# One queue for the loads after the first pair, the rows of w and u behind the first k, and the fill's state operations ahead of later sums, in an RWKV WKV kernel

## Chip, cores, metric

The kernel runs on one core of one Trainium2 chip. The metric is the device time of one execution in microseconds (us), lower is better. A run gets a state: on one core, "slow" is a run more than 1.5% above the fastest run of the same kernel. Ratios use fast runs alone.

## The reference

```python
# w, u: [256]; k, v: [16, 2048, 256] float32
for b in range(16):
    aa, bb, pp = 0, 0, -1e38
    for t in range(2048):
        kk, vv = k[b, t], v[b, t]
        ww = u + kk;  qq = max(pp, ww)
        e1, e2 = exp(pp - qq), exp(ww - qq)
        output[b, t] = (e1 * aa + e2 * vv) / (e1 * bb + e2 + 1e-8)
        ww = pp - w + kk;  qq = max(ww, kk)
        e1, e2 = exp(ww - qq), exp(kk - qq)
        aa, bb, pp = e1 * aa + e2 * vv, e1 * bb + e2, qq
```

## The kernel before

The sequence is cut into 16 chunks of 128 steps; a "pair" is four batches of one chunk, 128x1024 elements of k and as many of v (1.05 MB together), and there are 64 pairs. For each pair, VectorE rounds k (`km`), TensorE makes logarithms of weights from it and from w and u (`logs`), ScalarE takes exponentials into a ring (`exps`, L187 for the first nine pairs, the wide L189 after), and VectorE multiplies by v (`times_v`). The outputs come LAG = 9 pairs later: `den`, `recip`, `num`, `mult`, `store`. Beside this a state is carried from chunk to chunk: `sums` of four pairs, `copy_sums`, `turn`, logarithms `LL`, offsets, weights `G`, a product `CB`, `turn_back`, and `inject`, which copies the state (`cb`) with a small transfer `EZR<-cb` into one row of the ring, where `den` of the next chunk reads it. The loop's first nine slots, which fill the ring, are "the fill".

```python
    RING = 12; AHEAD = 6; LAG = 9
    ...
    for n in range(3):
        load(n, SP, SP)                    # k and v of pairs 0 to 2 in the SP queue
    for r, g0, x in ((0, 0, w), (1, 2, u)):
        K(SC.dma_start(out=wuf...))        # w and u in the ACT queue
    ...
    for n in range(3, AHEAD):
        load(n)                            # pairs 3 to 5, and later ones, in the POOL queue
    ...
    def inject(c):
        cb = small.tile([128, 128], BF16, tag="cb", name="cb")
        K(DVE.tensor_copy(cb, st.pop((c, "CT"))))
        r0 = 4 * c % RING
        for q in range(2):
            row = EZR[HS - 1:128:HS, 2 * q, r0, 0, 0:1]
            K(SP.dma_start(
                out=bass.AP(tensor=row.tensor, offset=row.offset, ap=[list(row.ap[0]), [1, 4 * 2 * D]]),
                in_=cb[HS * q:HS * q + HS, :]))
    ...
    for n in range(LAG):                   # the fill
        load(n + AHEAD)
        exps(n)
        logs(n + 1)
        if n:
            sums(n - 1)
        small_work(n, "act")               # state operations of this slot
        small_work(n, "nums")
        small_work(n, "pe")
        idle_matmuls(4, NUMB)
        small_work(n, "mid")
        small_work(n, "chain")
        times_v(n)
        cast_v(n + 1)
        round_k(n + 2)
    for n in range(LAG, NP):               # the steady part
        ...
```

## Time and profile before

| | before |
|---|---|
| time, median of 4 runs | 329.76 us (328.05 to 333.73) |
| span of the profiled run | 324.6 us |
| start to the first wide exponential (pair 9) | 54.73 us |
| from there to the second | 8.06 us |
| second to last wide exponential, 53 pairs | 229.15 us |
| last one to the end | 32.66 us |

The starts of the wide exponentials (128x2048, one per pair) are the best ruler of this kernel: they cut a run into fill, steady part and tail, and a gap of much more than 4.4 us between two of them is a stop. The granted clock was 1.00 until 20 us, 0.64 and 0.68 in the two stretches of 5 us from 20 to 30, 1.00 from 30 to 40 and 0.60 to 0.71 from 40 to 60; a matmul on k (L176, NLE) took 0.71 us near 23 and 46 us, and 0.46 from 9 to 15.

### The profile page before, as it was taken

The page shows a single profiled execution, that of the slowest core. Times are in us where ns is not written, and L with a number is a line of the kernel's source. Part 1 is how long each engine was busy: PE and PEld are TensorE (multiplying, and loading weights), DVE is VectorE, ACT ScalarE, POOL GpSimd, SP SyncE. Part 2 cuts the span into 40 slices and gives each one's busy share as a digit, 9 for nine tenths or more (in the row PEclk, how much of TensorE's full clock was granted, in tenths as well). Part 3 has the DMA queues.
Part 4 walks back from the last instruction along what each step waited for, and adds up shares of the span by engine and source line. Part 5 has one row for each costly group of instructions (what it writes and reads, how often), then busy time and mean ns, then how long its engine had stood idle before and what let it go on. Part 6 is the DMA issues. An engine that isn't in the chain of part 4 may idle for free.

```text
span 324.6 us, 4795 instructions
## 1 busy us (share of the span) xinstructions
PE 280.6 (86%) x1684; PEld 130.2 (40%) x1716; DVE 273.4 (84%) x547; ACT 258.7 (80%) x251; POOL 147.2 (45%) x204
## 2 busy tenths in 40 slices
PE   7839687899969999999989989898989999998781
PEld 2323343344434444444444444343434444444230
DVE  4835547599969999999999999999999999998652
ACT  1524543599868998989898989999898989898792
POOL 8824135046435454555553736364555543121231
PEclk9987957899998999999999999999999999999998
DMA  7999966469998999999999999999999999433566
GB/s 240 351 349 348 335 191 157 173 206 284 364 360 298 275 327 387 310 398 292 397 352 388 301 368 355 378 320 366 369 364 357 327 391 317 144 129 135 204 241 207
DMA packets 37914, 97.85 MB, mean 301 GB/s; under 512 B 5238, under 2 KB 16002, under 8 KB 37890
## 3 DMA queue, kind: packets, MB, share of 16 engines
q0 software_dynamic: 32016, 93.34, 86.2%
q1 hardware_dynamic: 5568, 3.93, 4.0%
q8 instruction: 13, 0.21, 0.3%
q10 hardware_dynamic: 306, 0.27, 0.3%
q14 instruction: 11, 0.09, 0.1%
HBM read 67.12 MB, written 33.55 MB: 310 GB/s over the span
## 4 chain that ended last, share of the span: by engine, by line
PE 60%; DVE 20%; DMA 12%; ACT 3%; issue 2%; SPq 1%; DVEq 0%; POOL 0%; ACTq 0%
PE PS L176 22%; PE PS L329 14%; DVE EZR L207 9%; PE PS L316 8%; DVE ot L335 8%; PE PS L171 7%; DMA vr<-in_v_dram 5%; DMA EZR<-cb 5%; PE PS L228 5%; ACT rd L322 2%; PE PS L372 2%; DMA kr<-in_k_dram 2%; PE PS L245 1%; DVE km L162 1%; DVE vb L202 1%
## 5 line engine op out<-in xcount | busy, mean ns | idle before, releaser
L340 POOL DMA_DIRECT2D out_dram<-ot x63 | 47.7, 757 | 143.3 <-DVE ot L335 84.1
L189 ACT ACTIVATE EZR<-PS 128x2048 bf16<-128x2048 f32 x55 | 102.7, 1867 | 10.7 <-PE PS L176 10.2
L335 DVE TENSOR_TENSOR ot<-PS,rd 128x512 f32<-128x512 f32 (+1 forms) x119 | 85.9, 724 | 15.6 <-PE PS L329 10.4
L207 DVE TENSOR_TENSOR EZR<-EZR,vb 128x2048 bf16<-128x2048 bf16 x64 | 78.3, 1224 | 4.3 <-ACT EZR L187 4.3
L322 ACT ACTIVATE rd<-PS 128x1024 f32<-128x1024 f32 (+1 forms) x65 | 65.5, 1007 | 8.4 <-PE PS L316 6.3
L324 ACT ACTIVATE rd<-rd 128x1024 f32<-128x1024 f32 (+1 forms) x65 | 68.0, 1046 | 2.0
L329 PE MATMUL PS<-EZR,LN 128*128 128x512 bf16 x126 | 48.2, 383 | 12.8 <-DVE ot L335 12.5
L176 PE MATMUL PS<-km,NLE 128*128 128x512 f32 x128 | 49.3, 467 | 10.6 <-DVE km L162 10.4
L61 POOL DMA_DIRECT2D kr<-in_k_dram x61 | 46.2, 758 | 20.9 <-DVE km L162 13.3
L162 DVE CAST km<-kr 128x1024 fp32r<-128x1024 f32 x64 | 47.2, 738 | 0.1
L316 PE MATMUL PS<-EZR,L 128*128 128x512 bf16 x127 | 37.9, 379 | 7.4 <-ACT rd L322 3.0
L176 PE MATMUL PS<-km,NLZ 128*128 128x512 f32 x128 | 41.9, 409 | 0.0
L69 POOL DMA_DIRECT2D vr<-in_v_dram x47 | 38.5, 819 | 6.0 <-DVE vb L202 5.2
L202 DVE CAST vb<-vr 128x1024 bf16<-128x1024 f32 x50 | 35.5, 710 | 5.2 <-DMA vr<-in_v_dram 5.2
L329 PE MATMUL PS<-EZR,IdN 128*128 128x512 bf16 x102 | 38.8, 381 | 0.2 <-issue 0.2
L316 PE MATMUL PS<-EZR,Id 128*128 128x512 bf16 x128 | 38.1, 379 | 0.1
L171 PE MATMUL PS<-WU,CO 32*128 32x512 f32 x256 | 34.5, 513 | 1.1 <-ACT EZR L189 0.4
L187 ACT ACTIVATE EZR<-PS 128x1024 bf16<-128x1024 f32 x18 | 17.4, 1022 | 22.4 <-PE PS L176 22.4
L176 PEld LDWEIGHTS PS<-km,NLE 128*128 128x128 f32 x128 | 20.1, 197 | 27.4 <-issue 13.9
L176 PEld LDWEIGHTS PS<-km,NLZ 128*128 128x128 f32 x128 | 25.2, 197 | 6.3
L228 PE MATMUL PS<-EZR,OH 128*32 128x256 bf16 x512 | 26.4, 284 | 0.0
L171 PEld LDWEIGHTS PS<-WU,CO 32*128 32x128 f32 x256 | 13.0, 187 | 30.3 <-issue 7.4
(58 smaller groups left out, 204.1 us busy)
## 6 DMA issues: line engine op xcount, KB each, us to landing
out_dram<-ot POOLq DMA_DIRECT2D x63, 512.0 KB, 6.5
kr<-in_k_dram POOLq DMA_DIRECT2D x61, 512.0 KB, 8.1
vr<-in_v_dram POOLq DMA_DIRECT2D x47, 512.0 KB, 8.8
vb<-in_v_dram POOLq DMA_DIRECT2D x14, 256.0 KB, 7.8
kr<-in_k_dram SPq DMA_DIRECT2D x3, 512.0 KB
vr<-in_v_dram SPq DMA_DIRECT2D x3, 512.0 KB
EZR<-cb SPq DMA_DIRECT2D x32, 16.0 KB
out_dram<-ot SPq DMA_DIRECT2D x2, 128.0 KB
```

What stands on the lines that cost most here:

```text
L61: K((kq or POOL).dma_start(out=kr, in_=src[0]))
L162: K(DVE.tensor_copy(km, kr_of.pop(n)))
L171: K(PE.matmul(half(n, q)[:, i, :], CO[g:g + 32, :], WU[g:g + 32, :], start=True, stop=False, tile_position=(g, 0), skip_group_check=True))
L176: K(PE.matmul(half(n, q)[:, i, :], (NLE, NLZ)[q], km[:, i, :], start=False, stop=True, skip_group_check=True))
L189: K(SC.activation(ez(n)[:, 0:2], PS[:, 0:4, :].rearrange("p (q i) x -> p q i x", q=2), ACT.Exp))
L207: K(DVE.tensor_mul(ez(n)[:, 2:4], ez(n)[:, 0:2], vb.unsqueeze(1).broadcast_to([128, 2, 2, D])))
L316: K(PE.matmul(DENB[:, i, :], mats[m], ez(n)[:, q, i, :], start=q == 0, stop=q == 1, skip_group_check=True))
L322: K(SC.activation(rd[:, i, :], DENB[:, i, :], ACT.Ln, scale=RS))
L324: K(SC.activation(rd[:, i, :], rd[:, i, :], ACT.Exp, scale=-1.0))
L329: K(PE.matmul(bank, mats[m], ez(n)[:, q, i, :], start=q == 2, stop=q == 3, skip_group_check=True))
L335: K(DVE.tensor_mul(o[:, i, :], bank, rd[:, i, :]))
L340: K(POOL.dma_start(out=out[4 * p:4 * p + 4, c * TC:(c + 1) * TC, :].rearrange("n t d -> t n d"), in_=OT.pop(n)))
```

## The change

The intent: deliver the first pairs in the order in which they are wanted, start the first pair earlier, and let the state's operations of the fill go before sums that they do not need. The diff, cut:

```diff
-    for n in range(3):
-        load(n, SP, SP)
-    for r, g0, x in ((0, 0, w), (1, 2, u)):
-        K(SC.dma_start(out=wuf...))
+    K(POOL.memset(wuf, 0.0))              # was on DVE
+    load(0, SP, SC)
+    load_row(SP, 0, 0, w)
+    load_row(SP, 1, 2, u)
     ... selects and iotas on POOL ...
-    for n in range(3, AHEAD):
+    for n in range(1, 3):
         load(n)
     ... selects of Lx and Sel, now behind these loads ...
+    for n in range(3, AHEAD):
+        load(n)
+    def out_matrices():                   # Id, IdN, L, LN: made at the end of slot 0
@@ the plan of the last chunk
-                    (s + 2, "pe", turn_back), (s + 2, "last", inject)]
+                    (s + 3, "turn", turn_back), (s + 3, "first", inject)]
@@ the fill
-        if n:
+        if n and n % 4 == 0:
             sums(n - 1)
         small_work(n, "act")
         small_work(n, "nums")
+        small_work(n, "mid")
+        small_work(n, "chain")
+        if n % 4:
+            sums(n - 1)
         small_work(n, "pe")
         idle_matmuls(4, NUMB)
-        small_work(n, "mid")
-        small_work(n, "chain")
         times_v(n)
@@ the tail
         small_work(n, "turn")
+        small_work(n, "first")
```

More of the change, by code (lines that the diff above doesn't have):

```diff
@@ L91, with load_row @@
     Sel = consts.tile([128, 3, 2, 2, 4, 2], F32, tag="Sel", name="Sel")
+    def load_row(eng, r, g0, x):
+        K(eng.dma_start(out=wuf.rearrange("(g r) n d -> r g n d", r=32)[r, g0:4], in_=bass.AP(
+            tensor=x.tensor, offset=x.offset, ap=[[0, 4 - g0], [0, 2], list(x.ap[0])])))
+    K(POOL.memset(wuf, 0.0))
     fill(M1, -1.0)
-    fill(wuf, 0.0)
-    for n in range(3):
-        load(n, SP, SP)
-    for r, g0, x in ((0, 0, w), (1, 2, u)):
-        K(SC.dma_start(out=wuf.rearrange("(g r) n d -> r g n d", r=32)[r, g0:4], in_=bass.AP(
-            tensor=x.tensor, offset=x.offset, ap=[[0, 4 - g0], [0, 2], list(x.ap[0])])))
+    fill(I1, 0.0)
+    load(0, SP, SC)
+    load_row(SP, 0, 0, w)
+    load_row(SP, 1, 2, u)
     K(SC.preload_act_table_set("natural_log_exp_and_others"))
-    fill(I1, 0.0)
     fill(idle, 0.0)
-    fill(Lx, 1.0)
     select(M1, GE, 0.0, -1, -1, [[1, 128]])
@@ L110 @@
         select(COf, NE, 1.0, -32 * g - 1, 1, [[0, 128]])
-    select(Lx, GE, 0.0, -1, -1, [[1, 128]])
-    for h in range(2):
-        select(Lx, NE, 1.0, -(HS * h + HS - 1), 1, [[0, 128]])
-    for n in range(3, AHEAD):
+    for n in range(1, 3):
         load(n)
@@ L123 @@
     K(DVE.tensor_tensor(NLZ, NLE, I1, ALU.add))
+    fill(Lx, 1.0)
     fill(Sel, 0.0)
-    for j, r in ((0, 0), (1, 8), (2, 64)):
-        for h in range(2):
-            select(Sel[:, j, h], NE, 1.0, -r - h, 1, [[-16, 2], [-2, 4], [-32, 2]])
     fill(OH, 0.0)
@@ L132 @@
     K(DVE.tensor_copy(CO, COf))
+    select(Lx, GE, 0.0, -1, -1, [[1, 128]])
     for h in range(2):
-        fill(Lx[HS * h:HS * h + HS, HS * (1 - h):HS * (2 - h)], 0.0)
-    mats = {}
-    for name, x, f in (("Id", I1, 1.0), ("IdN", I1, RS), ("L", Lx, 1.0), ("LN", Lx, RS)):
-        mats[name] = matrix(name, BF16)
-        K(DVE.tensor_single_scalar(mats[name], x, f, op=ALU.mult))
-    mats["OH"], mats["Sel"] = OH, Sel.rearrange("p a h n c i -> p (a h) n (c i)")
-    WU = consts.tile([128, D], F32R, tag="WU", name="WU")
-    K(DVE.tensor_copy(WU, wuf.rearrange("p n d -> p (n d)")))
+        select(Lx, NE, 1.0, -(HS * h + HS - 1), 1, [[0, 128]])
+    for j, r in ((0, 0), (1, 8), (2, 64)):
+        for h in range(2):
+            select(Sel[:, j, h], NE, 1.0, -r - h, 1, [[-16, 2], [-2, 4], [-32, 2]])
+    for n in range(3, AHEAD):
+        load(n)
+    WU = consts.tile([128, D], F32R, tag="WU", name="WU")
+    mats = {"OH": OH, "Sel": Sel.rearrange("p a h n c i -> p (a h) n (c i)")}
+    def out_matrices():
+        for h in range(2):
+            fill(Lx[HS * h:HS * h + HS, HS * (1 - h):HS * (2 - h)], 0.0)
+        for name, x, f in (("Id", I1, 1.0), ("IdN", I1, RS), ("L", Lx, 1.0), ("LN", Lx, RS)):
+            mats[name] = matrix(name, BF16)
+            K(DVE.tensor_single_scalar(mats[name], x, f, op=ALU.mult))
     EZR = consts.tile([128, 4, RING, 2, D], BF16, tag="EZR", name="EZR")
@@ L374 @@
     idle_matmuls(16, MISC)
+    K(DVE.tensor_copy(WU, wuf.rearrange("p n d -> p (n d)")))
     round_k(0)
@@ L395 @@
         round_k(n + 2)
+        if n == 0:
+            out_matrices()
     for n in range(LAG, NP):
```

## The prediction

> **What bounds the kernel now.** I read the page first: VectorE (DVE), TensorE (PE) and ScalarE (ACT) are each busy for 80 to 86% of the span, so no average names a bound. The stretches do.
>
> ```profile
> 10.00:15.00 5.00, 4.16 (x21) 1.84 (x19) 3.98 (x10) 3.88 (x4) 4.01 (x7) 1.00 1.05 348
> 15.00:20.00 5.00, 2.76 (x19) 1.28 (x20) 1.06 (x1) 1.94 (x2) 1.50 (x2) 1.00 1.05 349
> ...
> 50.00:55.00 5.00, 2.67 (x17) 1.23 (x13) 4.78 (x7) 0.55 (x2) 2.87 (x2) 0.71 0.52 102
> ...
> 60.00:65.00 5.00, 3.46 (x23) 1.13 (x22) 2.08 (x4) 4.20 (x5) 0.00 (x0) 1.00 0.25 87
> ...
> 140.00:180.00 40.00, 37.28 (x242) 17.16 (x247) 38.95 (x77) 36.69 (x35) 20.59 (x28) 1.00 1.05 364
> ```
>
> Columns: length, busy time of PE, weight loads, DVE, ACT, POOL, granted clock, DMA share, GB/s. From 100 to 290 us DVE is busy for about 98%, one pair costs 4.28 us (the 128x2048 exponentials start 17.1 us apart per four), and nothing in that loop is edited. The fill, up to the first 128x2048 exponential at 54.73 us, is different: DVE idles there while the DMA engines are saturated at 350 GB/s until 40 us, and then the DMA engines idle too (102 and 87 GB/s). So the fill is first starved by loads and later by something else. The waits up to 66 us name both:
>
> ```profile
> DVE nF L256 <- ACT LL L250: 5.6, 2, 3.6
> DVE vb L202 <- DMA vr<-in_v_dram: 5.2, 1, 5.2
> DVE cb L302 <- PE PS L296: 3.3, 1, 3.3
> DVE WU L141 <- DMA wuf<-in_u_dram: 2.3, 1, 2.3
> ACT LL L250 <- PE PS L228: 1.8, 1, 1.8
> DVE tb L276 <- PE PS L228: 1.6, 1, 1.6
> ```
>
> (total us, times, longest.) The chain that ended last passes through the second of these, and the timeline shows its end:
>
> ```profile
> 3.85 17.44 DMA vr<-in_v_dram
> ...
> 17.41 0.51 PE L171 MATMUL PS<-WU,CO 32*128 32x512 f32 x4
> 21.31 0.69 DVE L202 CAST vb<-vr 128x1024 bf16<-128x1024 f32 x1 [5.25 <-DMA vr<-in_v_dram]
> 22.66 1.22 PE L176 MATMUL PS<-km,NLE 128*128 128x512 f32 x2 [4.74 <-DVE km L162]
> ```
>
> The v of pair 2 lands at 21.3 us. By then some 350 GB/s x 18.8 us = 6.6 MB had moved, over six pairs of 1.05 MB, because pairs 0 to 2 go in one queue and 3 to 5 beside them in another: bandwidth goes to data not yet wanted. A last place is in the tail, where PE, in its order, waits for the last state product:
>
> ```profile
> 302.30 0.40 PE L296 MATMUL PS<-Id,CB 128*128 128x128 bf16 x4 [1.31 <-DVE CB L280]
> 303.65 1.22 DVE L335 TENSOR_TENSOR ot<-PS,rd 128x1024 f32<-128x1024 f32 x1 [0.63 <-PE PS L329]
> 304.97 1.02 ACT L322 ACTIVATE rd<-PS 128x1024 f32<-128x1024 f32 x1 [1.59 <-DVE ot L335]
> ```
>
> [...] the sixth transfer of the first queue (3.1 MB in all) lands only when 6.6 MB have moved. [...] LL reads the turned sums in one half of a bank and still waits for the next sums (L228) written to the other half, 1.8 us. [...] Here a load costs POOL 0.75 us typically and up to 1.1, so I count it as a risk of tenths. [...]
>
> **The change, part by part.**
>
> *Start.* k0 alone heads the SP queue, w and u follow at once, v0 is alone in the ACT queue, and pairs 1 and up are issued by POOL. k0 and v0 together are 1.05 MB, 3.0 us from the first data at about 2.5 us: landed at about 5.5 to 6. w and u, 12 KB, ride behind: about 6.3. WU (0.57, at 8.30 before) is then ready at about 6.9 and km0 (0.72) at 7.5; the first L176 matmul, 9.57 before, comes at about 7.5. The wuf memset moves to POOL; at 0.48 us on DVE, I allow 0.5 to 1 there, ahead of 1.9 us of selects and iotas. Loads of pairs 1 and 2 leave POOL between about 3.3 and 6.3 us (four of 0.75), when k0 and v0 still flow; pair 3 leaves at about 10, and data for 2.5 + 3 x 3.0 = 11.5 us is queued by then. So no gap in the data.
>
> *One queue in order.* Pair n now lands at about 2.5 + 3.0(n+1): v2 at 11.5 to 12.5 and k3 at 13 to 14, where DVE had v2 at 21.3. From there the slot takes the larger of DMA 3.0, DVE 1.22 + 0.69 + 0.69 = 2.6 and PE in its order: rows 0.51, steps 1.35, sums 0.40, four idle matmuls 1.04 and gaps, 3.36 as between 27.03 and 30.39 us. Walking the slots: DVE has times_v(0) at 10.1, v1 and k2 cast by 12.4, the four output matrices moved there 1.15 (as at 4.86 to 6.0), times_v(1) at 13.5, k3 rounded at 15.9, k4 at 18.3. PE's steps for pairs 3, 4, 5 then start at 15.9, 19.2 and 22.6, the last two by 3.36. Before, those of pair 5 started at 30.82: 8.2 us saved, of which I count 7.5, as k4 and k5 land within a microsecond of being wanted.
>
> *State ahead of later sums.* In slot 5, LL no longer waits for L228: 1.8 us, all of it on the way LL, offsets, times_v, rounding of k7, since DVE sat 3.6 us for LL. In slot 6, tb loses its 1.6 us; it may pay some of it to G, whose exponential ends about 0.4 us after exps(6): 1.5 counted. In slot 7, turn_back only passes one set of sums, 0.5 us; the rest of cb's 3.3 us is logs(8), which stays ahead. Slot 8 keeps its old order: 0. Sum 3.8. PE's clock adds something: with no 4.7 us hole before pair 3, matmuls that ran 1.4 to 1.5 times longer near 23, 46, 52 and 56 us may run full; 1.0 counted of a possible 2.5.
>
> *Tail.* The four matmuls of pair 56 (0.88 us) go ahead of turn_back, into the 1.31 us in which PE waits for CB. cb is still ready at about 303.0, so the multiplication at 303.65 can come at about 303.0, and the reciprocals behind it, which wait for it, move with it: 0.6.
>
> Sum: 7.5 + 3.8 + 1.0 + 0.6 = 12.9 us. Part of it is given back below.
>
> **The rivals.** (a) *The steady part pays it back.* It needs 97.85 MB / 64 = 1.53 MB per 4.28 us, 357 GB/s[...], and the slack of the DMA engines between 40 and 75 us is worth some 16 us by the GB/s row (5.7 MB below 350). The earlier start uses 12 of it. The state's small transfer EZR<-cb then lands later: it took 9.6 us at 85.8 and cost one slot 3.4 us (exponentials 7.78 instead of 4.38 apart). One or two more such stops would leave 6 to 9 us of the gain, 322 to 325 us. Against: in steady state loads are issued some six pairs ahead and land within 7 to 9 us, without growth from 120 to 260 us, and slot 9 is long enough (8 us, one pair of loads) for the backlog to drain. I take off 0.9 for it. (b) *The fill becomes compute-bound at once*: with the idle matmuls at 3.36 us per slot, PE and not loads then sets it, and any landing delay adds. If slots 1 to 5 took 4.0 instead of 3.4, the gain would be 9 to 10, so 321. (c) *The loads were hidden anyway and the gain is nil*: then the chain would not have 17.44 us on v2 with DVE idle for 5.2 and all engines at zero between 18 and 20 us. I give this 2%. (d) *POOL issues too late*, after memset and selects: each microsecond of gap in the data costs as much; at most 2.
>
> **Range and chances.** 330.8 - 12.9 + 0.9 = 318.8 us, called 319. If all goes well (clock 2.5, full 8.2, a stop of 3.4 gone) 312 to 313; if (a) comes fully, 325. The three runs of before spread over 5.7 us, which is most of the rest. Faster by over 2% means below 324.2, a gain of 6.6, half of what I count: 0.88. Within 2%: 0.11. Slower by over 2%: 0.01.
>
> **What would show it right or wrong.** Right: v2 lands by 13 us and the wait of 5.2 us for it is gone; the first L176-kind matmul before 8.5; the first 128x2048 exponential at 41 to 44 us instead of 54.73; waits of LL and tb for sums gone; 350 GB/s until about 40 us and a shorter dip after it; 4.28 us per pair as before; the span from the last rows matmul to the end shorter by about 0.6. Wrong: the first such exponential after 47 (the fill has another bound), or on time but with new waits for EZR<-cb, pairs over 4.4 us apart or DVE waiting for loads after 60 us (rival a), or the first data gap between 6 and 12 us (rival d).

## The result, and the profile after

The changed kernel takes 320.57 us, median of 4 runs (318.93 to 333.11), against 329.76; it and all kernels below gave correct results. The ratio is 0.972, 95% interval 0.965 to 0.979: the mean time of this kernel's fast runs over that of the other's of the same rounds, so not quite the ratio of the medians. It is faster by 2.8%, about 9 us, and the median lies within 2 us of the predicted 319.

The run with the first profile was a slow one (333.11 us). So the same kernel was profiled again on another chip (e1 below); that run was fast, 314.81 us. Its stretches, with the columns as before (length, PE, weight loads, DVE, ACT, POOL, clock, DMA share, GB/s):

```profile
10.00:15.00 5.00, 4.28 (x28) 2.15 (x27) 4.49 (x10) 3.37 (x5) 4.98 (x9) 1.00 1.02 329
15.00:20.00 5.00, 4.69 (x31) 2.18 (x29) 4.54 (x7) 2.85 (x3) 5.00 (x5) 1.00 1.00 346
50.00:55.00 5.00, 4.09 (x25) 1.74 (x24) 4.02 (x9) 4.97 (x6) 1.29 (x2) 0.97 0.69 238
60.00:65.00 5.00, 4.84 (x35) 2.48 (x34) 5.00 (x7) 4.92 (x7) 3.00 (x5) 1.00 1.02 276
140.00:180.00 40.00, 37.74 (x250) 17.58 (x249) 39.26 (x77) 37.08 (x35) 21.66 (x29) 1.00 1.05 365
```

From 15 to 20 us DVE is now busy for 4.54 of 5 us instead of 1.06, at the same 346 to 349 GB/s: the same traffic, in a useful order. The steady stretch has not changed. The waits of the first 55 us of the same run (total us, times, longest), with those for v of pair 2 and of LL and tb for the sums gone:

```profile
DVE WU L378 <- DMA wuf<-in_u_dram: 2.8, 1, 2.8
PE PS L319 <- DMA EZR<-cb: 2.8, 1, 2.8
DVE nF L259 <- ACT LL L253: 2.6, 2, 1.7
...
DVE cb L305 <- PE PS L299: 1.5, 1, 1.5
```

The second of these lines is new. The timeline of the same run shows it at the end of the fill:

```profile
7.69 0.73 PE L179 MATMUL PS<-km,NLE 128*128 128x512 f32 x2
...
22.18 0.73 PE L179 MATMUL PS<-km,NLE 128*128 128x512 f32 x2
...
35.67 1.12 SPq L309 DMA_DIRECT2D EZR<-cb  x2
...
40.49 1.87 ACT L192 ACTIVATE EZR<-PS 128x2048 bf16<-128x2048 f32 x1
...
46.86 1.01 PE L319 MATMUL PS<-EZR,L 128*128 128x512 bf16 x2 [2.81 <-DMA EZR<-cb]
...
48.76 1.02 ACT L325 ACTIVATE rd<-PS 128x1024 f32<-128x1024 f32 x1 [6.23 <-PE PS L319]
```

The first matmul on k comes at 7.69 us (9.57 before), the one of pair 5 at 22.18 (30.82), the first wide exponential at 40.49 (54.73): the fill is 14.2 us shorter. But the first state, issued at 35.67, lands only at 46.8, PE waits for it before the first output, and the second wide exponential comes 10.29 us after the first, instead of 8.06.

Cut at the wide exponentials, in us ("four copies" is e2 and e4, explained below):

| stretch | before | after, fast (e1) | after, slow | before, four copies (e4) | after, four copies (e2) |
|---|---|---|---|---|---|
| to the first | 54.73 | 40.49 | 40.97 | 56.08 | 40.79 |
| first to second | 8.06 | 10.29 | 9.98 | 8.06 | 6.51 |
| second to last | 229.15 | 230.09 | 248.20 | 225.54 | 225.14 |
| last to the end | 32.66 | 32.23 | 32.25 | 32.52 | 31.76 |
| span | 324.6 | 313.1 | 331.4 | 322.2 | 304.2 |

The fill of the slow run is as short as that of the fast one. All that the slow run loses, 18.1 us, lies between the second and the last wide exponential. There, six gaps of 6.6 to 8.2 us stand among gaps of about 4.4, at every eighth pair. The waits of the slow run, over its whole span:

```profile
PEld L319 <- DMA EZR<-cb: 21.1, 8, 3.7
PE PS L319 <- DMA EZR<-cb: 19.8, 8, 3.3
```

and of the fast one:

```profile
PE PS L319 <- DMA EZR<-cb: 8.0, 3, 2.8
...
PEld L319 <- DMA EZR<-cb: 6.2, 2, 3.2
```

(Weight loads and matmuls of one stop both have a line; they are not to be added.) So the two runs differ by the number of stops for the state's small transfer, and the question is what that transfer waits for.

### The profile page after: what moved, and what is told of

It is laid out like the page before. It is cut to its first block, busy times and chain, and to the rows that moved or that the text cites.

```text
span 331.4 us, 4824 instructions
## 1 busy us (share of the span) xinstructions
PE 282.1 (85%) x1716; PEld 128.5 (39%) x1716; DVE 273.7 (83%) x546; ACT 260.0 (78%) x251; POOL 152.8 (46%) x209
## 2 busy tenths in 40 slices
DMA packets 36378, 97.85 MB, mean 295 GB/s; under 512 B 5238, under 2 KB 13954, under 8 KB 36354
## 4 chain that ended last, share of the span: by engine, by line
PE 48%; DMA 29%; DVE 14%; ACT 4%; issue 2%; POOL 0%; DVEq 0%; SPq 0%; ACTq 0%; POOLq 0%
DMA EZR<-cb 26%; PE PS L179 14%; PE PS L332 12%; PE PS L319 11%; DVE EZR L210 5%; PE PS L174 5%; DVE ot L338 5%; PE PS L231 4%; ACT rd L325 3%; DMA kr<-in_k_dram 2%; DMA wuf<-in_u_dram 1%; ACT EZR L190 1%; DVE km L165 1%; DVE vb L205 1%; PE PS L248 1%
## 5 line engine op out<-in xcount | busy, mean ns | idle before, releaser
L319 PE MATMUL PS<-EZR,L 128*128 128x512 bf16 x128 | 40.3, 398 | 22.7 <-DMA EZR<-cb 19.8
L332 PE MATMUL PS<-EZR,LN 128*128 128x512 bf16 x128 | 50.2, 392 | 10.6 <-DVE ot L338 9.8
L61 POOL DMA_DIRECT2D kr<-in_k_dram x63 | 49.7, 789 | 6.9 <-DVE km L165 1.9
L179 PE MATMUL PS<-km,NLE 128*128 128x512 f32 x128 | 47.9, 456 | 4.4 <-DVE km L165 4.2
L332 PE MATMUL PS<-EZR,IdN 128*128 128x512 bf16 x128 | 49.8, 389 | 0.0
L165 DVE CAST km<-kr 128x1024 fp32r<-128x1024 f32 x64 | 48.5, 760 | 0.0
L179 PE MATMUL PS<-km,NLZ 128*128 128x512 f32 x128 | 41.0, 402 | 0.0
L319 PE MATMUL PS<-EZR,Id 128*128 128x512 bf16 x128 | 40.4, 399 | 0.0
L190 ACT ACTIVATE EZR<-PS 128x1024 bf16<-128x1024 f32 x18 | 17.4, 1021 | 14.4 <-PE PS L179 14.4
L319 PEld LDWEIGHTS <-L 128*128 128x128 bf16 x128 | 12.0, 99 | 40.9 <-DMA EZR<-cb 21.1
L179 PEld LDWEIGHTS PS<-km,NLE 128*128 128x128 f32 x128 | 19.4, 191 | 21.4 <-issue 14.8
```

The costliest lines, as they stand in the source:

```text
L61: K((kq or POOL).dma_start(out=kr, in_=src[0]))
L165: K(DVE.tensor_copy(km, kr_of.pop(n)))
L179: K(PE.matmul(half(n, q)[:, i, :], (NLE, NLZ)[q], km[:, i, :], start=False, stop=True, skip_group_check=True))
L319: K(PE.matmul(DENB[:, i, :], mats[m], ez(n)[:, q, i, :], start=q == 0, stop=q == 1, skip_group_check=True))
L332: K(PE.matmul(bank, mats[m], ez(n)[:, q, i, :], start=q == 2, stop=q == 3, skip_group_check=True))
```

## The experiments

Two theories of the stops were open. M: an inject lands late because of its shape, two copies of two partitions each, 128 packets of 256 B in all. Q: the transfer lands late since there is a backlog of loads, however it is cut. And there was a rival to stops altogether, R: the steady part is slower for another reason.

### e1: the changed kernel again

> The changed kernel as it is, once more, to get a profile of a fast run (the first profile fell in a slow one: 331.4 us, with the first wide exponential at 40.97 us instead of 54.73 but six stops of 3 to 4 us for EZR<-cb). Theory S (stops): the fill keeps its gain of 13.8 us in every run, and runs differ only by the number of stops for EZR<-cb: a fast run of 318 us has two or three of them (7 to 9 us), since 324.6 - 13.8 - 0.6 would be 310. Rival R (the steady part is slower for another reason): a fast run has no more than the one stop that the kernel before had, and the missing 8 us are spread over pairs of more than 4.28 us or lie in the tail.

Measured: 314.81 us in the profiled run, where S had 318 for a fast one; the timed ones 320.29, 323.94 and 324.14. The profile has three stops (second gap 10.29; later 6.22 and 6.38 us), the steady gaps are 3.94 to 4.54 as ever, and the tail is 0.4 us shorter. Theory S holds, R falls. That the other three runs have more stops is likely from their times, but they have no profile.

### e2: the inject as four copies of one partition

```diff
         for q in range(2):
-            row = EZR[HS - 1:128:HS, 2 * q, r0, 0, 0:1]
-            K(SP.dma_start(out=bass.AP(..., ap=[list(row.ap[0]), [1, 4 * 2 * D]]),
-                           in_=cb[HS * q:HS * q + HS, :]))
+            for h in range(2):
+                p = HS * h + HS - 1
+                row = EZR[p:p + 1, 2 * q, r0, 0, 0:1]
+                K(SP.dma_start(out=bass.AP(..., ap=[list(row.ap[0]), [128, 32], [1, 128]]),
+                               in_=cb[HS * q + 32 * h:HS * q + 32 * h + 32, :]))
```

> The changed kernel with the state's small transfer EZR<-cb issued as four copies of one partition (32 rows of 256 B) instead of two copies of two partitions. Theory M [...] lands in 2 to 4 us instead of 7 to 11. Then no stop is left and the time is 308 to 312 us in every run. Rival Q (backlog): the transfer lands late because all DMA engines have a backlog of loads and stores, however it is cut; then the stops stay, or grow a little as the last of four copies is issued 1 us later, and the time stays at 319 to 321 or above. Rival R: no stop to take away, 318 to 321.

Measured: 306.33 us median (305.37 to 307.07), all four runs within 0.6%; ratio to the kernel before 0.927 (0.918 to 0.936). (The record's rule classes the ratios of e2, e3, e4, e7, e9 and e10 as unclear; here the slowest run of e2 is 21 us below the fastest of the seven runs of the kernel before in the same rounds.) No stop is left in the profile (waits for EZR<-cb: 0.2 us in all), the second gap is 6.51 us. M's time was met and passed, and as the cause of the stops Q falls. One number of M was missed: the copies land 5.4 us after their issue in the median, not the estimated 2 to 4.

```profile
DMA to landing us min/median/max: 1.8/5.4/6.5
```

The packets can be counted on the page. The first of these lines is of the slow run of the changed kernel, the second of e2:

```profile
DMA packets 36378, 97.85 MB, mean 295 GB/s; under 512 B 5238, under 2 KB 13954, under 8 KB 36354
```

```profile
DMA packets 37338, 97.85 MB, mean 322 GB/s; under 512 B 6198, under 2 KB 14914, under 8 KB 37314
```

Both move the same 128 packets of 256 B per inject, and e2 has 960 more packets under 512 B, of 4 B in the trace. On how many DMA engines a copy ran is not shown. What the records do show is the packets' times. From the start of the first of an inject's 128 packets to the end of the last, in us, in order (taken from the packet records of the trace):

```
after, fast (e1):  8.7 1.7 1.9 2.2 1.9 1.6 1.9 1.8 1.6 4.0 7.3 1.9 8.0 1.1 1.1 1.1
after, slow:       8.2 1.4 8.4 1.3 7.1 1.7 8.1 6.0 8.0 5.1 8.0 2.0 7.9 1.1 1.1 1.2
after, e2:         2.7 2.1 2.5 4.6 2.5 3.0 2.6 2.4 3.0 3.2 2.5 2.4 3.6 2.1 (the last two run together)
```

With the two copies an inject's packets mostly take either about 1 to 2 us, or 7 to 9 us (4.0, 5.1 and 6.0 also occur), and the three stops of e1 belong to the three entries above 7. By its own record a small packet takes 0.018 us (median), and a 4096 B packet of the loads 0.18 (mean): 128 small ones add to 2.3 us, so most of 8 us is not their own time. In the first long one of e1, from 39.99 to 45.9 us, 63 small packets start, mostly in twos about 0.2 us apart. That is about the time of one packet of the loads and one small one (0.18 and 0.018 us), but what a small packet waits for is not shown, since the records do not name the engine.

The same records say when an inject is long. During the injects of 5 us and more, 16.1 to 17.4 packets of loads and stores are in flight on the average; during those of up to 2.7 us, at most 15.5 (all 48 injects of the profiles before, after slow and e1; the one of 4.0 us has 15.6). So the long ones are those with more traffic in flight. Why there is less at one inject than at the next is not shown.

One part of the delay does not depend on the shape. The first small packet starts 4.3 us after the issue in e1 (35.67 to 39.99 us) and 4.4 us in e2 (35.89 to 40.33), when 336 GB/s are moved, but 1.4 us in the kernel before at 49.19, when 203 are (49 to 51 us). Most of the 5.4 us that e2's copies still take is this part, which M had left out.

### e3: one more pair of delay

```diff
-    LAG = 9
+    LAG = 10
-    TURNS = 9
+    TURNS = 10
```

> The changed kernel with the outputs one pair further behind (LAG and TURNS 10 instead of 9), so that EZR<-cb has 4.3 us more before it is wanted. Theory S: stops of 3 to 4 us vanish, for one more pair in the fill and one more in the tail instead of one in the steady part (estimate 2.9 + 2.15 - 4.28 = +0.8 us): 310 to 313 us. Rival R: nothing but the +0.8: 319 to 322.

Measured: 308.80 us (307.44 to 309.92), no wait for EZR<-cb in the list of waits, no gap over 4.6 us after the twelfth pair. So the stops vanish either by landing sooner (e2) or by waiting later (e3). It is 2.5 us behind e2 (means 308.74 and 306.28), more than the 0.8 estimated; the tail alone is 34.0 instead of 31.8 us.

### e4: the kernel before with the four copies

> The kernel before with the same four copies as in e2. Theory M: its stop of 3.4 us at pair 18 and those that its slower runs have vanish: 321 to 323 us (profiled span about 321) and a small spread. The difference to e2 is then the change without its stops: 13.8 in the fill, 0.6 in the tail and the 2 us that the slot of the first outputs lost, 12 to 15 us. Rival Q: 328 to 331 as before.

Measured: 320.29 us median; fast runs 317.80, 319.84, 320.73 (mean 319.5), and a profiled run of 323.86 that counts as slow. No stop is in the profile. So the kernel before loses to the shape of the copies as well: its fast runs on that chip have a mean of 330.4. That all of these 11 us were stops is likely, not shown, since its one profile has a single stop of 3.4 us. With the four copies the change is worth 319.5 - 306.3 = 13.2 us, where its own form gave 9.1 on the first chip. On this chip its own form has one run that counts as fast (e1, 314.81 us: 15.6 us below the 330.4), and the other three have a mean of 322.8 (7.6 us); the difference between 13.2 and 9.1 is no firmer than that. The spread was not small, which the expectation had wrong: 6 us remain, and the profile puts its own excess in the fill (first wide exponential at 56.08 instead of 54.73).

### e5, e6, e7, e8: the parts, on the base of the four copies

e5 is e2 with the loop of the fill and the plan of the last chunk as before; e6 and e7 are e4 with one of these as after; e8 is e2 with

```diff
     for n in range(1, 3):
-        load(n)
+        load(n, SP, SP)
```

> The four copies of e2 (so that no stops blur it) with the start and the one queue of loads alone: the state operations of the fill and the last inject stand as in the kernel before. Base e4: 319.5 us mean of its fast runs, first wide exponential at 56.08 us in its profile; all parts together (e2): 306.3 and 40.79. Terms as predicted: the loads give 7.5, and a warm clock 1.0 more, so 310 to 312 us, with the first wide exponential at 45 to 48 us and waits of LL and tb for the sums back. Rival L (the loads alone do it all and the state order adds nothing, because DVE waits elsewhere): 306 to 308.

> The four copies with the state operations of the fill ahead of later sums alone, loads and tail as before. Term as predicted: 3.8 us, so 315 to 317 us against 319.5, first wide exponential at 51 to 52.5. If the loads set the fill whatever the order (rival L): 318 to 320.

> The four copies with the last turn_back and inject moved behind the sums of pair 56 alone. Term as predicted: 0.6 us, seen best as the distance from the last wide exponential to the end of the span (32.5 us in e4, 31.8 in e2): 31.7 to 31.9 here, time 318 to 320. If the wait for CB only moves elsewhere: 32.5.

> All parts with the four copies (e2, 306.3 us), but the loads of pairs 1 and 2 issued on the SP queue again, behind the rows of w and u, with pairs 3 and up on the POOL queue as ever. Theory F (two queues share the bandwidth, so that pair 2 is late): v of pair 2 lands near 21 us again, DVE waits 3 to 5 us for it, the first wide exponential comes at 44 to 46 us instead of 40.8, and the time is 309 to 311. Rival: what helped was the early start (rows behind the first k, first matmul at 7.9 instead of 9.6 us) and the later output matrices, and the queues do not matter: 306 to 307, first wide exponential at 41.

Measured (fast runs; e4 and e2 ran on another chip than e5 to e8):

| | mean, us | median of all | first wide exponential | first to second | last to the end |
|---|---|---|---|---|---|
| e4: none | 319.5 | 320.29 | 56.08 | 8.06 | 32.5 |
| e5: loads alone | 312.0 | 311.88 | 44.63 | 8.77 | 32.5 |
| e6: state order alone | 314.4 | 315.13 | 50.65 | 7.75 | 32.4 |
| e7: tail alone | 319.4 | 321.88 | 56.18 | 8.04 | 31.7 |
| e2: all | 306.3 | 306.33 | 40.79 | 6.51 | 31.8 |
| e8: all, but pairs 1 and 2 in the SP queue | 313.5 | 313.43 | 48.58 | 6.51 | 31.8 |

By the times, loads give 7.5 us and the state order 5.0; the tail's 0.8 us shows only in the profile, since its times vary by more. Together that is 13.3, and e2 has 13.2. The profiles give more for the loads (11.5 us to the first wide exponential), probably because the profiled run of e4, which counts as slow, had a long fill. The exact fit of the sum is partly luck, since the base e4 ran on another chip: as shares of the kernel before in the same rounds, e5 and e6 are 2.05% and 1.31% below e4, and e2 is 3.99%. Rival L falls: the state order adds its part. Of the expectations, the times of e5 and e7 were met by the fast means; e6 is 0.6 us below its range and e8 2.5 us above theory F's, and the first wide exponentials of e5 and e6 (0.4 us early each) and of e8 (2.6 late) lie outside theirs. In e5 the waits for sums are back:

```profile
DVE tb L279 <- PE PS L231: 1.8, 1, 1.8
ACT LL L253 <- PE PS L231: 1.8, 1, 1.8
```

e8 settles the queues. Everything else of the change is in it, its first exponential starts at 9.10 us, and yet v of pair 2, issued at 4.27 us, is late again by as much as before. VectorE's timeline of e8, then that of e1 at the same pair:

```profile
12.22 0.68 DVE L205 CAST vb<-vr 128x1024 bf16<-128x1024 f32 x1
14.70 0.69 DVE L165 CAST km<-kr 128x1024 fp32r<-128x1024 f32 x1 [1.80 <-DMA kr<-in_k_dram]
...
21.79 0.69 DVE L205 CAST vb<-vr 128x1024 bf16<-128x1024 f32 x1 [4.36 <-DMA vr<-in_v_dram]
```

```profile
11.58 0.78 DVE L205 CAST vb<-vr 128x1024 bf16<-128x1024 f32 x1
12.28 0.87 DVE L165 CAST km<-kr 128x1024 fp32r<-128x1024 f32 x1
...
15.10 0.69 DVE L205 CAST vb<-vr 128x1024 bf16<-128x1024 f32 x1
```

It costs 7.2 us against e2 (on another chip), more than theory F's 3 to 5, and about all that the loads' part gives: what the early start gives by itself is too small to be seen in these times.

### e9 and e10: two tries at a better version

e9 is e2 with LAG and TURNS 8; e10 is e2 with `idle_matmuls(2, NUMB)` in the fill. Both ran on a third chip.

> The four copies (e2, 306.3 us) with the outputs one pair less behind (LAG and TURNS 8). Theory S says that a stop is the landing time of the small copies less the time they have: with LAG 8 some 2.6 us from their first issue (85.8 to 88.4 in the kernel before), the last of four copies leaves 1.5 us after the first and lands some 2 us later, so 1 to 1.5 us stop for each of 15 injects, 15 to 22 us against 0.8 saved: 318 to 328 us, with waits for EZR<-cb in nearly every fourth pair. If the copies land within the time, 305 to 306, and a version better than e2.

> The four copies (e2, 306.3 us, wide exponential at 40.8) with two idle matmuls a fill slot instead of four. If PE's own order sets the fill's slot (rival b of the prediction, 3.36 us), each of nine slots loses 0.5 us: wide exponential at 37 to 38, time 302 to 304. If VectorE (busy 13.3 of 15 us from 10 to 25 us) or the loads (349 GB/s) set it: within 0.5 us of e2, or up to 1.5 us slower where the clock drops.

e9: 385.41 us (379.25 in its fast run), ratio 1.18. The direction was right, the size far off. The waits of e9:

```profile
PE PS L321 <- DMA EZR<-cb: 57.8, 15, 5.4
```

Fifteen stops, 3.9 us each in the mean, because the copies land after 5.4 to 7.3 us (pieces of the chain) and not after 3.5 as estimated; and a pair with a stop takes about 10 us instead of 4.4, 2 us more than the wait, in which the clock also drops (mean 0.918).

e10: 308.35 us (fast runs 306.71 to 309.07), 1.8 us slower than e2 by the means, which is less than the means of the kernel before differ between the two chips (328.5 and 330.4); the spans of the profiles differ by 3.2 us. Until 25 us both have a clock of 1.00, and the first matmul on k of pair 5 starts at 22.36 us (22.42 in e2), so the idle matmuls did not set the fill's slot there. Then the clock falls, to 0.89 from 25 to 40 us, and the first wide exponential is at 41.18. From 40 to 48 us, e10, then e2:

```profile
40.00:48.00 8.00, 7.46 (x36) 3.32 (x35) 4.79 (x12) 2.46 (x4) 2.85 (x4) 0.57 1.10 322
```

```profile
40.00:48.00 8.00, 6.38 (x43) 2.83 (x43) 5.02 (x12) 5.01 (x6) 2.50 (x4) 1.00 1.10 323
```

PE does fewer matmuls in more time (36 in 7.46 us against 43 in 6.38), and the second gap is 8.70 instead of 6.51 us. By the profiles the idle matmuls earn their place. e2 stays the best version: 306.3 us, 7% below the kernel before and 4% below the changed one (306.3 against 320.1, the means of fast runs on two chips).

## Why the prediction was right, and where not

*The loads.* The mechanism is shown: two queues share the bandwidth. In the kernel before, when v of pair 2 had landed at 21.3 us, 3.15 MB had come in the SP queue and 3.35 MB in the POOL queue (packet records): it came with pairs 3 to 5. In e8 it landed 17.49 us after its issue at 4.27. One queue in order removes the wait (5.2 us before, none in e1). The walk through the slots had pairs 3, 4 and 5 start at 15.9, 19.2 and 22.6 us; the slow profile has 16.75, 19.62 and 22.48. That the last one fits is partly luck: pair 3 came 0.85 us later than said, and the two slots after it took 2.87 us each instead of the 3.36 that PE's order was to need (e10 shows that it does not set them). The term was 7.5; e5 has 7.5. In e1, v of pair 2 landed at 12.8 us (issued at 5.59, 7.2 us to landing), by 13 as said. What the walk gave to the early start (2 us at the first matmul, 1.9 measured) showed no gain by itself in e8, since the next pairs' loads decide.

*The state order.* Counted 3.8, with up to 1.0 for the clock beside it; e6 has 5.0. LL and tb lost the 1.8 and 1.6 us as said. The mis-sized place is slot 7, where I said that turn_back only passes one set of sums and saves 0.5: DVE's wait for it fell from 3.3 to 1.5 (e6). The rest of that wait was the logarithms of pair 8, whose two groups of matmuls took 1.22 and 1.05 us in e4, where the clock was 0.66 (40 to 50 us), and 0.73 and 0.62 in e6, where it was 1.00 (40 to 46 us). So the clock's gain, which I put down to the hole before pair 3, comes also with the state order alone; with the loads alone (e5) the wait is 2.0.

*The tail.* Counted 0.6; 0.8 in e7. As said, the multiplication no longer waits for the sums of its pair behind turn_back:

```profile
291.23 0.40 PE L299 MATMUL PS<-Id,CB 128*128 128x128 bf16 x4 [0.45 <-DVE CB L283]
...
291.87 1.21 DVE L338 TENSOR_TENSOR ot<-PS,rd 128x1024 f32<-128x1024 f32 x1
...
293.18 1.02 ACT L325 ACTIVATE rd<-PS 128x1024 f32<-128x1024 f32 x1 [0.86 <-DVE ot L338]
```

(e1's timeline.) The multiplication starts 0.64 us after turn_back, against 1.35 before.

*The sum.* 12.9 us were counted without rivals; 13.2 were measured where no stops blur it. The time came out closer than the gain: with 0.9 given back 12.0 us were predicted, from a base of 330.8 (the median of three runs), and 9.1 measured, from 329.2 (the mean of the fast ones). The base was 1.6 us too high, and that part of the fit is luck.

*Rival a, the mis-sized term.* I took 0.9 us off for stops; the change gives 9.1 by its fast runs instead of 13.2, so about 4 were given back (a difference of means of two chips, see e4). The prediction's own sign of this rival was there: the first wide exponential on time, even early (40.49 us, not 41 to 44), but a new wait for EZR<-cb. Two steps of that paragraph failed. That "slot 9 is long enough" for the backlog to drain looked at the loads alone. The first state is issued at 35.67 us, while 336 GB/s are moved (35 to 47 us); before, it was issued at 49.19, when the traffic had fallen to 179 and then 102. In e1 it landed after 11.15 us, and den of pair 0 waited: the second gap is 10.29 us in e1 and 6.51 in e2, 3.8 us, as much as nearly the whole 4 (that the later stops then cost both kernels about alike is argued, not shown). And the stop of the kernel before was read as one event of one profile, 3.4 us; e4 shows that the shape of the copies costs its fast runs about 11 us on the average (330.4 against 319.5). I also called it a matter of backlog; e2 moves the same 97.85 MB with the copies in the same queue in 304.2 us instead of 313.1 (spans of e2 and e1) without a stop, so it was the shape of the small copies.

*Rivals b, c, d.* PE's order does not set the fill's first slots (e10); the loads were not hidden; in e1 POOL's memset took 0.53 us, its first load left at 3.20 us, the issue of a k took it 0.79 us in the mean against 0.76 before (two in the fill of the slow run took 1.74 and 1.61), and the data show no more of a gap than 311 GB/s between 5 and 6 us (229 in its worst 0.3 us).

*Left open:* why fewer packets are in flight at one inject than at the next, on how many engines a copy runs, why 4 us pass under load before an inject's first packet, and why the fill of the kernel before varies by a few microseconds from run to run. The "slow" runs here are, where a profile exists, runs with more stops or a longer fill; whether that holds of all is not shown.

## What to carry to other kernels

Look at order, not at bandwidth, where an engine starves while DMA is saturated (before, from 15 to 20 us: DVE busy for 1.06 of 5 us at 349 GB/s): here the loads put in two queues arrived together, and the one wanted first came with later ones. Before an earlier start of a loop is counted in full, ask which small transfer was issued into quiet before and will now be issued into traffic (here the first state: 1.4 us from issue to its first packet at 203 GB/s, 4.3 us at 336). And try another shape for a small copy on a critical path: here four copies of one partition instead of two of two were worth about 14 us to the changed kernel (fast runs of two chips; 8.5 against the one fast run on the same chip) and 11 to the one before, about as much as the change itself.
